# The beginning of a SwiGLU stage: a third pair's first product in front, weight sums behind the norm's lo parts, TensorE's products in order

## The chip, the cores and the metric

The kernel runs on one core of one Trainium2 chip. The metric is the device time of one execution in microseconds (us), the median of several runs. TensorE (PE) multiplies matrices, VectorE (DVE) and ScalarE (ACT) work on elements, GpSimd (POOL) does a part of that and issues some transfers, SyncE (SP) issues most loads.

## The reference

One layer of a residual block over 1024 tokens with 1024 channels: a mixing part, and then a SwiGLU feed-forward network (FFN) of width 2816. Only the FFN's beginning matters here:

```
mix = einsum('bsd,de->bse', g_a * y_a + g_b * y_b, w_o[l])
x = x + g1 * mix
h2 = rms_norm(x, norm_ffn_g[l]) * (1.0 + sc2) + sh2
a, bgate = jnp.split(jnp.einsum('bsd,df->bsf', h2, w_ffn_in[l]), 2, axis=-1)
x = x + g2 * jnp.einsum('bsf,fd->bsd', jax.nn.silu(a) * bgate, w_ffn_out[l])
return rms_norm(x, final_norm_g)
```

`a` and `bgate` have 2816 columns each, which are 22 blocks of 128.

## The kernel before

Everything is kept with channels on the 128 partitions and tokens along the free dimension, in two halves of 512 tokens. A float32 product is made of three matmuls on operands that are split into a hi part (rounded) and a lo part (the rest): weight hi by operand hi, weight hi by operand lo, weight lo by operand hi. These are lines 283, 284 and 286 in `mm3`. A weight tile of 128x1024 is split by `split_w`: ACT casts the hi (`wh`, L205), DVE subtracts to get the lo (`wl`, L206). An operand tile of 128x512 is split by `t_split` in the same way (L322 on ACT, L323 on DVE).

The FFN's first matrix is multiplied by a scheme of Strassen's kind (Winograd's form). A "dual" `d` is a pair of column blocks; it takes seven products instead of eight, in the order `PRODUCTS = "1265734"`. Each product has two parts p of 4 x 3 = 12 matmuls, 24 in all. Products 1, 6, 7 and 4 add up in the banks `x`, product 2 in `y`, 5 and 3 in `z`, two PSUM banks each. There are eleven duals.

- Product 1 takes h2 of the first half of the tokens, channel blocks 0 to 3; product 2 the same half, blocks 4 to 7. Only these two need nothing of the second half.
- Product 6 takes `t2`, products 5, 7, 3 and 4 take `t1`, `t3`, `b22` and `t4`: sums of blocks of both halves, split in hi and lo.
- Weights: products 1 and 2 take blocks 11 and 12 as loaded. Products 6, 5 and 7 need sums of blocks (L228, L229, L230), product 3 one more (L232); these are 128x1024 operations on DVE. `dual_units(..., early)` makes the seven weights of a dual. When `early` is true, each block is loaded when its product comes, so blocks 11, 12 and 22 are loaded twice; otherwise all four are loaded at product 1.

The loads go to a ring of five 128x1024 raw buffers (a sixth is added after `norm_2_last`), the split weights to three `wh` and three `wl` buffers. `next_w` writes the weights of the product two places further before it hands out the present one.

The stage before writes x1 of the second half and sums its squares. Then the order written in the code is: (0,1), written (dual, product); the second half's norm begins on PE (L404, between the two parts of (0,1)), ACT (L333) and DVE (L338 to L340), which gives `r2`; then (0,2), (1,1) and (1,2), with `norm_2_half(k, r2)` ahead of each; the fourth `norm_2_half`; `norm_2_last`; then (0,6), (0,5), (0,7), (0,3), (0,4), the same five of dual 1, and from dual 2 on seven products each. `norm_2_half` normalises block k and k + 4 (L824 on DVE, L831 on ACT), makes t2 (L850, L327) and splits it. `norm_2_last` makes and splits t1, t3 (L863), b22 and t4, in that order. So DVE has to do the norm, the operands and the weights here.

`in_evac` reads the banks: products 1, 6, 5 are copied by ACT (L905); 2, 7, 3 are added by DVE (L907, L910, L914 and L915); 4 goes through ACT's Silu (L918) and DVE (L919). After the last product of a dual, `hid_set` splits seven tiles into three staging tiles and POOL stores them.

The order in the code isn't the order on an engine. A scheduler places the instructions of each engine when the kernel is built, by the order in the code and by its own estimate of when operands are ready. Each engine then works in that order. `tc.issue_after(ins)` puts the instructions that are written under it, those on the engine of `ins`, behind `ins`.

PSUM has eight banks, six in the pool `ps` (`ps_tile`) and two in `ps2` (`ps2_tile`). Before the change, x and z of every dual come from `ps`, and y from `ps2`, except for dual 1, whose y comes from `ps` (`y_tile`).

Of the kernel before, what the change touches and what calls it, by code (L numbers as in the profile page):

```python
# [37 lines left out]
ALU = mybir.AluOpType  # L38
# [53 lines left out]

PRODUCTS = "1265734"

GROUP, GROUPS = 3, 3
# [10 lines left out]
def block_kernel(ctx: ExitStack, tc: tile.TileContext, x0, xT, c, vecs, ada, w_first, w_plain, w_duals,  # L108
                 w_short, w_conf, w_o, w_fi, w_fo, w_last, outT):
    nc = tc.nc  # L110
# [27 lines left out]
    def ps_tile(name):  # L138
        return psp.tile([P, H], F32, tag="ps", name=name)
# [13 lines left out]
    def f32(t):  # L153
        return t.bitcast(F32)
# [29 lines left out]
    def raw_tile(n=1024):  # L184

        raws.append(raws.pop(0))
        return raws[-1].tile([P, 1024], F32, tag="raw", name="raw")[:, :n]

    def load(src, n=1024):
        raw = raw_tile(n)  # L190
        nc.sync.dma_start(raw, src)
        return raw
# [6 lines left out]
    def split_w(raw, n, after=(), lo_engine=nc.vector):  # L199
        wh = whp.tile([P, 1024], F32R, tag="wh", name="wh")[:, :n]  # L200
        wl = wlp.tile([P, 1024], F32R, tag="wl", name="wl")[:, :n]
        with ExitStack() as order:
            for ins in after:
                order.enter_context(tc.issue_after(ins))
            nc.scalar.copy(wh, raw)  # L205
            lo = lo_engine.tensor_tensor(wl, raw, f32(wh), ALU.subtract)  # L206
        if n == T and lo_engine is nc.gpsimd:
            pool_los.append(lo.ins)
        return wh, wl

    def dual_units(mats, n, early=False, eng=nc.vector):

        a = {}

        def get(*blocks):
            for b in blocks:
                a[b] = load(mats[("11", "12", "21", "22").index(b)], n)

        def unit(m):
            if early:  # L220
                get(*{"1": ("11",), "2": ("12",), "6": ("21", "22", "11"), "3": ("12",), "4": ("22",)}.get(m, ()))
            elif m == "1":
                get("11", "12", "21", "22")
            if m in "12":
                return split_w(a["1" + m], n, (), eng)
            if m == "6":
                a["s1"] = a["22"] if early else raw_tile(n)
                eng.tensor_tensor(a["s1"], a["21"], a["22"], ALU.add)  # L228
                eng.tensor_tensor(a["21"], a["21"], a["11"], ALU.add)  # L229
                eng.tensor_tensor(a["11"], a["11"], a["s1"], ALU.add)  # L230
            elif m == "3":
                eng.tensor_tensor(a["12"], a["12"], a["11"], ALU.add)  # L232
            return split_w(a[{"6": "11", "5": "s1", "7": "21", "3": "12", "4": "22"}[m]], n, (), eng)

        return {m: (lambda m=m: unit(m)) for m in PRODUCTS}


    plan = [None] * KC
# [8 lines left out]
    def next_w(ahead=AHEAD):  # L247

        fetch(ahead + 1)
        return ready.pop(0)  # L250
# [24 lines left out]
    def mm3(outs, wsl, w, xs, first, last, again=False):  # L275

        if w[1] is None:
            for ps, x in zip(outs, xs):
                mm3.ins = nc.tensor.matmul(ps, w[0][:, wsl], x, start=first, stop=last).ins
            return  # L280
        wh, wl = w[0][:, wsl], w[1][:, wsl]
        for ps, (xh, xl) in zip(outs, xs):
            nc.tensor.matmul(ps, wh, xh, start=first, stop=False, skip_group_check=again)  # L283
            nc.tensor.matmul(ps, wh, xl, start=False, stop=False, skip_group_check=again)  # L284
        for ps, (xh, _) in zip(outs, xs):
            mm3.ins = nc.tensor.matmul(ps, wl, xh, start=False, stop=last, skip_group_check=again).ins  # L286
# [5 lines left out]
            mm3(outs, slice(k * P, k * P + P), w, [act[k][h] for h in hs], k == 0, k == KC - 1)  # L292
        return outs

    def product(banks, m, t, evac=None, between=None, y_tile=ps2_tile):

        w = next_w()
        b = {"1": "x", "6": "x", "7": "x", "4": "x", "2": "y", "5": "z", "3": "z"}[m]
        n = len(t)
        for p in range(2):  # L300
            if m in "125":
                banks[b, p] = (y_tile if b == "y" else ps_tile)(b)
            ps = banks[b, p]
            for k in range(n):
                c0 = (p * n + k) * P
                mm3([ps], slice(c0, c0 + P), w, [t[k]], m in "125" and k == 0, k == n - 1, m in "6734")
            if evac:
                evac(p, m, ps)
            if between and p == 0:
                between()  # L310
# [9 lines left out]

    def t_split(src, hi, lo):
        nc.scalar.copy(hi, src)  # L322
        nc.vector.tensor_tensor(lo, src, f32(hi), ALU.subtract)  # L323

    def minus(out, a, b):

# [61 lines left out]
    x = {}  # L388
# [22 lines left out]
    def uc_tile(name, n=T + CK - 1, dt=F32):  # L411
        return ucp.tile([P, T + CK - 1], dt, tag="uc", name=name)[:, :n]
# [24 lines left out]
    for k in range(0, KC, 2):  # L437
        t = uc_tile("x0", T)
# [62 lines left out]
    KH = KC // 2  # L501
# [228 lines left out]
    banks = [[ps_tile(b) for _ in range(2)] for b in "xyz"]  # L730
# [104 lines left out]
    ts = {m: [None] * (KC // 2) for m in PRODUCTS}  # L835
# [9 lines left out]
    def norm_2_half(k, r2):  # L845

        h2_of(k, 1, r2)
        b22 = h2_of(k + KH, 1, r2)
        b11, b12 = (x1[k][:, s] for s in halves)
        nc.vector.tensor_tensor(b11, b11, b12, ALU.subtract)  # L850
        t2.append(hl_tile("t2", dt=F32))
        minus(t2[k], b11, b22)
        ts["6"][k] = t_pair("t2")
        t_split(t2[k], *ts["6"][k])

    def norm_2_last():

        for k in range(KH):
            ts["5"][k] = t_pair("t1")
            t_split(x1[k][:, halves[0]], *ts["5"][k])  # L860
        for k in range(KH):
            b12, b22 = x1[k][:, halves[1]], x1[k + KH][:, halves[1]]
            nc.vector.tensor_tensor(b12, b22, b12, ALU.subtract)  # L863
            ts["7"][k] = t_pair("t3")
            t_split(b12, *ts["7"][k])
        for k in range(KH):
            ts["3"][k] = t_pair("b22")
            t_split(x1[k + KH][:, halves[1]], *ts["3"][k])
        b21 = [x1[k + KH][:, halves[0]] for k in range(KH)]
        for k in range(KH):  # L870
            minus(b21[k], t2[k], b21[k])
        for k in range(KH):
            ts["4"][k] = t_pair("t4")
            t_split(b21[k], *ts["4"][k])

    sums = {}
    for h in range(2):
# [6 lines left out]


    N_IN = FC // 2
    in_units = [dual_units([w_fi[d, m] for m in range(4)], 1024, d < 2) for d in range(N_IN)]
    in_order = [(d, m) for d in range(2) for m in "12"] + [(d, m) for d in range(2) for m in PRODUCTS[2:]]
    in_order += [(d, m) for d in range(2, N_IN) for m in PRODUCTS]
    plan += [in_units[d][m] for d, m in in_order]  # L890
    ha = {}
    in_banks = [{} for _ in range(N_IN)]

# [6 lines left out]
    def in_evac(d):  # L900
        def evac(p, m, ps):
            f = 2 * d + p
            if m in "165":
                ha[f, m] = t = in_tile(d, m)
                nc.scalar.copy(t, ps)  # L905
            elif m == "2":
                nc.vector.tensor_tensor(ha[f, "1"], ps, ha[f, "1"], ALU.add)  # L907
            elif m == "7":
                t = ha[f, "5"]
                nc.vector.tensor_tensor(t, ps, t, ALU.add)  # L910
                nc.scalar.activation(t, t, AF.Silu, scale=-1.0)
            elif m == "3":
                t = ha[f, "6"]
                nc.vector.tensor_tensor(t, ps, t, ALU.add)  # L914
                nc.vector.tensor_tensor(t, t, ha[f, "5"], ALU.mult)  # L915
            else:
                t = gip.tile([P, H], F32, tag="g", name="g4")
                nc.scalar.activation(t, ps, AF.Silu, scale=-1.0)  # L918
                nc.vector.tensor_tensor(t, t, ha[f, "1"], ALU.mult)  # L919
                ha[f, "4"] = t  # L920
        return evac
# [40 lines left out]
        to[g, m] = [t_load((g * GROUP + i, m)) for i in range(GROUP)]  # L962

    def in_product(d, m):
        product(in_banks[d], m, ts[m], in_evac(d), y_tile=ps_tile if d == 1 else ps2_tile)
        if d == N_IN - 1:
            group_load(0, m)

# [3 lines left out]

    r2 = None
    product(in_banks[0], "1", ts["1"], in_evac(0), norm_2_start)
    r2 = rstd_end(*r2)
    for i, (d, m) in enumerate(in_order[1:4]):
        norm_2_half(i, r2)
        in_product(d, m)
    norm_2_half(KH - 1, r2)
    norm_2_last()  # L980
    close(*phase_1)
    raws.append(open_pool("raw_a", 1, side="right", stack=ctx)[1])
    x1ap = open_pool("x1a", 2, side="right", stack=ctx)[1]
    phase_2 = [open_pool("gi", 7), open_pool("stage", 3, side="right")]
    gip, stagep = (p for _, p in phase_2)
    for d, m in in_order[4:]:
        in_product(d, m)
        if m == PRODUCTS[-1]:
            if 2 <= d < 6:
                for i in range(40 + 2 * (d - 2), 42 + 2 * (d - 2)):  # L990
                    modulation(i, x1ap.tile([P, T], F32, tag="x1", name="ada"))
            hid_set(d)
# [31 lines left out]
    for g in range(GROUPS):  # L1024
        for d in range(2):
            banks = {}
# [177 lines left out]
```

## Time and profile before

| | us |
|---|---|
| median of 3 runs | 1505.06 |
| lowest and highest run | 1504.25, 1505.3 |
| the profiled execution | 1502.96 |
| its span in the trace | 1501.2 |
| first product of the FFN begins on PE | 841.26 |
| first product 6 begins on PE | 864.07 |

The mean granted clock of TensorE over the whole execution is 0.995 of full speed. All rows that follow are of that one profiled execution; times in them are counted from the start of its span. A row of a timeline has the start, the duration, the engine, the line, the operation, output<-inputs, the shape and the count, and in brackets the idle time of the engine before it and what ended it. A matmul's row is longer than the step from one matmul to the next, since matmuls overlap; the step is read from the starts. The same holds, by a little, for DVE.

### The profile page before, as it was taken

What the parts mean: (1) busy time and instruction counts of PE and PEld (TensorE: products, weight loads), DVE (VectorE), ACT (ScalarE), POOL (GpSimd) and SP (SyncE); (2) the same over time, 40 slices, a digit from 0 to 9 for tenths busy, and PEclk for the clock granted to TensorE, in tenths of its full rate; (3) what the DMA queues carried; (4) which work ended last, traced back from release to release, by engine and by line L of the source; (5) the groups of instructions that cost most, each with busy time, mean ns of one, the idle gap of its engine ahead of it and who ended that gap; (6) DMA issues with size and microseconds to landing.
All of it is one profiled execution on the core that took longest, in us unless ns stands there. A gap on an engine that the chain in (4) does not pass through costs nothing.

```text
span 1501.2 us, 17711 instructions
## 1 busy us (share of the span) xinstructions
PE 1469.3 (98%) x6455; PEld 1202.0 (80%) x6455; DVE 1141.0 (76%) x1569; ACT 623.1 (42%) x896; POOL 538.2 (36%) x467
## 2 busy tenths in 40 slices
PE   6999999999999999999999989999999999999997
PEld 2788888888888788887788868888888888888887
DVE  7994999887887984777767789776666665667755
ACT  4653433443343353244345454444444443222235
POOL 0037777777767773410121001111000016444005
PEclk9999999999999999999999989999999999999999
DMA  9522223232222268555765337544444449998403
GB/s 352 207 64 74 94 71 112 70 108 75 98 71 85 99 261 299 167 175 175 231 207 183 126 98 236 200 169 153 152 149 150 153 148 351 364 324 256 141 28 112
DMA packets 82697, 247.24 MB, mean 165 GB/s; under 512 B 9521, under 2 KB 11697, under 8 KB 82610
## 3 DMA queue, kind: packets, MB, share of 16 engines
q1 hardware_dynamic: 41776, 137.91, 27.4%
q0 software_dynamic: 36944, 95.44, 19.2%
q10 hardware_dynamic: 3890, 12.78, 2.2%
q8 instruction: 50, 0.82, 0.2%
q14 instruction: 37, 0.30, 0.1%
HBM read 183.69 MB, written 62.39 MB: 164 GB/s over the span
## 4 chain that ended last, share of the span: by engine, by line
PE 93%; DVE 4%; issue 1%; ACT 1%; DMA 1%; POOL 0%; POOLq 0%; ACTq 0%; DVEq 0%
PE x L286 11%; PE x L284 11%; PE x L283 10%; PE z L283 7%; PE z L284 7%; PE z L286 7%; PE y L284 6%; PE y L283 6%; PE y L286 6%; PE ya L284 2%; PE mix L286 2%; PE mix L284 2%; PE ya L283 2%; PE ya L286 2%; PE mix L283 2%; PE yb L283 2%
## 5 line engine op out<-in xcount | busy, mean ns | idle before, releaser
L205 ACT CAST wh<-raw 128x1024 fp32r<-128x1024 f32 (+2 forms) x257 | 259.4, 1010 | 482.8 <-PE z L284 122.0
L206 POOL TENSOR_TENSOR wl<-raw,wh 128x1024 fp32r<-128x1024 f32 x92 | 227.2, 2471 | 131.1 <-ACT wh L205 130.9
L206 DVE TENSOR_TENSOR wl<-raw,wh 128x1024 fp32r<-128x1024 f32 (+2 forms) x165 | 188.4, 1142 | 52.7 <-ACT wh L205 50.0
L671 DVE SCALAR_TENSOR_TENSOR c<-diff,vec,c 128x512 f32<-128x512 f32 x248 | 178.6, 751 | 3.3
L930 POOL DMA_DIRECT2D hid<-stage x71 | 37.9, 534 | 358.7 <-DVE stage L323 353.0
L283 PE MATMUL x<-th,wh 128*128 128x512 f32 x240 | 93.4, 389 | 0.0
L284 PE MATMUL x<-tl,wh 128*128 128x512 f32 x240 | 93.4, 389 | 0.0
L286 PE MATMUL x<-th,wl 128*128 128x512 f32 x240 | 93.4, 389 | 0.0
L671 DVE SCALAR_TENSOR_TENSOR c<-u,wsum,c 128x512 f32<-128x512 f32 x112 | 84.1, 751 | 1.8
L264 DVE CUSTOM_DVE_ANT_0 raw<-raw,cs,vec 128x1024 f32<-128x1024 f32 x24 | 35.5, 1486 | 50.6 <-DMA raw<-in_ada 50.6
L283 PE MATMUL z<-th,wh 128*128 128x512 f32 x168 | 65.4, 389 | 0.0
L284 PE MATMUL z<-tl,wh 128*128 128x512 f32 x168 | 65.4, 389 | 0.0
L286 PE MATMUL z<-th,wl 128*128 128x512 f32 x168 | 65.4, 389 | 0.0
L228 POOL TENSOR_TENSOR raw<-raw 128x1024 f32<-128x1024 f32 x12 | 29.8, 2482 | 95.0 <-DVE wl L206 94.2
L322 ACT CAST stage<-g 128x512 fp32r<-128x512 f32 x62 | 38.3, 621 | 52.0 <-DMA hid<-stage 25.1
L323 DVE TENSOR_TENSOR stage<-g,stage 128x512 fp32r<-128x512 f32 x62 | 42.5, 688 | 20.5 <-ACT stage L322 20.4
L956 POOL DMA_DIRECT2D th<-hid x71 | 38.1, 537 | 52.0 <-PE x L286 28.3
L283 PE MATMUL yb<-zsh,wh 128*128 128x512 f32 x128 | 50.0, 391 | 2.8 <-DVE gb L793 2.8
L283 PE MATMUL x<-t2h,wh 128*128 128x512 f32 x120 | 47.7, 400 | 5.1 <-ACT wh L205 2.8
L286 PEld LDWEIGHTS x<-th,wl 128*128 128x128 f32 x240 | 45.1, 188 | 9.4
L283 PEld LDWEIGHTS x<-th,wh 128*128 128x128 f32 x240 | 45.1, 188 | 9.3
L284 PEld LDWEIGHTS x<-tl,wh 128*128 128x128 f32 x240 | 45.1, 188 | 9.3
(1012 smaller groups left out, 4263.8 us busy)
## 6 DMA issues: line engine op xcount, KB each, us to landing
hid<-stage POOLq DMA_DIRECT2D x71, 512.0 KB, 4.0
raw<-in_w_fi SPq DMA_DIRECT2D x50, 512.0 KB, 4.3
raw<-in_w_duals SPq DMA_DIRECT2D x48, 512.0 KB, 3.5
th<-hid POOLq DMA_DIRECT2D x71, 256.0 KB, 5.9
tl<-hid POOLq DMA_DIRECT2D x71, 256.0 KB, 6.0
ada<-in_ada SPq DMA_DIRECT2D x24, 512.0 KB, 5.8
raw<-in_ada SPq DMA_DIRECT2D x24, 512.0 KB, 4.5
raw<-in_w_fo SPq DMA_DIRECT2D x24, 384.0 KB, 6.2
```

The costliest lines, as they stand in the source:

```text
L205: nc.scalar.copy(wh, raw)
L206: lo = lo_engine.tensor_tensor(wl, raw, f32(wh), ALU.subtract)
L228: eng.tensor_tensor(a["s1"], a["21"], a["22"], ALU.add)
L264: nc.vector.tensor_tensor_reduce(out=raw, in0=raw, in1=cs, scale=1.0, scalar=col(V_ADA, b), op0=ALU.mult, op1=ALU.add, accum_out=modc(b),)
L283: nc.tensor.matmul(ps, wh, xh, start=first, stop=False, skip_group_check=again)
L284: nc.tensor.matmul(ps, wh, xl, start=False, stop=False, skip_group_check=again)
L286: mm3.ins = nc.tensor.matmul(ps, wl, xh, start=False, stop=last, skip_group_check=again).ins
L322: nc.scalar.copy(hi, src)
L323: nc.vector.tensor_tensor(lo, src, f32(hi), ALU.subtract)
L671: tap.ins = nc.vector.scalar_tensor_tensor(out=out, in0=src[:, s : s + H], scalar=wt, in1=acc, op0=ALU.mult, op1=ALU.add).ins
L930: nc.gpsimd.dma_start(hid_dram[key], s)
L956: nc.gpsimd.dma_start(t, hid_dram[key][:, s])
```

## The change

A constant `FRONT = 3` says how many duals have their first products in front. The order becomes (0,1), (0,2), (1,1), (1,2), (2,1), then the rest of dual 0, of dual 1 and of dual 2 (from product 2), and from there as before. Dual 2's weights are made with `early`, too. A `norm_2_half` stands ahead of each of the four products behind (0,1), (2,1) among them. The evacuation of (2,1) is left to the time just ahead of (2,2), so x of dual 2 stays in its two banks until then.

y of dual 1 comes from `ps2` now, as all y do, and z of dual 0 from `ps2` instead of `ps`.

The weight of product 6 of duals 1 and 2 is written under `issue_after` with the last DVE instruction of `norm_2_last` (the last t4l): its three sums and its lo stand behind it in DVE's order. The products 6 of duals 1 and 2 are written under `issue_after` with the last matmul of the product before them in the code, so PE's order can't put them ahead of it.

```
+FRONT = 3
...
-    def product(banks, m, t, evac=None, between=None, y_tile=ps2_tile):
+    def product(banks, m, t, evac=None, between=None, y_tile=ps2_tile, z_tile=ps_tile):
...
-                banks[b, p] = (y_tile if b == "y" else ps_tile)(b)
+                banks[b, p] = {"x": ps_tile, "y": y_tile, "z": z_tile}[b](b)
...
-        nc.vector.tensor_tensor(lo, src, f32(hi), ALU.subtract)
+        t_split.ins = nc.vector.tensor_tensor(lo, src, f32(hi), ALU.subtract).ins
...
             t_split(b21[k], *ts["4"][k])
+        norm_2_last.ins = t_split.ins
...
-    in_units = [dual_units([w_fi[d, m] for m in range(4)], 1024, d < 2) for d in range(N_IN)]
-    in_order = [(d, m) for d in range(2) for m in "12"] + [(d, m) for d in range(2) for m in PRODUCTS[2:]]
-    in_order += [(d, m) for d in range(2, N_IN) for m in PRODUCTS]
-    plan += [in_units[d][m] for d, m in in_order]
+    in_units = [dual_units([w_fi[d, m] for m in range(4)], 1024, d < FRONT) for d in range(N_IN)]
+    in_order = [(d, m) for d in range(FRONT) for m in "12"][: 2 * FRONT - 1]
+    in_order += [(d, m) for d in range(N_IN) for m in PRODUCTS if (d, m) not in in_order]
+
+    def in_unit(d, m):
+
+        if d in range(1, FRONT) and m == "6":
+            with tc.issue_after(norm_2_last.ins):
+                return in_units[d][m]()
+        return in_units[d][m]()
+
+    plan += [lambda d=d, m=m: in_unit(d, m) for d, m in in_order]
...
-        product(in_banks[d], m, ts[m], in_evac(d), y_tile=ps_tile if d == 1 else ps2_tile)
+        product(in_banks[d], m, ts[m], in_evac(d) if (d, m) != (FRONT - 1, "1") else None,
+                z_tile=ps2_tile if d == 0 else ps_tile)
...
-    for i, (d, m) in enumerate(in_order[1:4]):
+    for i, (d, m) in enumerate(in_order[1 : 2 * FRONT - 1]):
         norm_2_half(i, r2)
         in_product(d, m)
-    norm_2_half(KH - 1, r2)
     norm_2_last()
...
-    for d, m in in_order[4:]:
-        in_product(d, m)
+    for d, m in in_order[2 * FRONT - 1 :]:
+        if (d, m) == (FRONT - 1, "2"):
+            for p in range(2):
+                in_evac(d)(p, "1", in_banks[d]["x", p])
+        if d in range(1, FRONT) and m == "6":
+            with tc.issue_after(mm3.ins):
+                in_product(d, m)
+        else:
+            in_product(d, m)
```

## The prediction

> **What bounds the kernel now.** I read the page's busy times first, then TensorE's (PE's) waits, then stretches of the FFN's beginning, then the order of PE's, VectorE's (DVE's) and ScalarE's (ACT's) instructions there.
>
> ```profile
> span 1501.2 us, 17711 instructions
> PE 1469.3 (98%) x6455; PEld 1202.0 (80%) x6455; DVE 1141.0 (76%) x1569; ACT 623.1 (42%) x896; POOL 538.2 (36%) x467
> ```
> ```profile
> PE yb L283 <- DVE gb L793: 2.8, 2, 1.6
> PE x L283 <- ACT wh L205: 2.8, 1, 2.8
> PE x L283 <- ACT t2h L322: 2.3, 1, 2.3
> PE x L286 <- DVE wl L206: 1.0, 1, 1.0
> ```
> PE is busy nearly throughout, so only its gaps and its slow phases can be won; work of other engines counts where PE waits for it. Three of these waits lie in the stage that the change touches (x is a bank of products 1, 6, 7, 4; t2 the operand of product 6). The stretches around them (columns: length, busy time with count for PE, its weight loads, DVE, ACT, POOL; granted clock; DMA share; GB/s):
>
> ```profile
> 841.26:868.39 27.13, 27.13 (x117) 21.36 (x115) 25.58 (x35) 15.30 (x23) 0.54 (x1) 1.00 0.33 104
> 868.39:876.20 7.81, 5.41 (x16) 3.80 (x16) 7.76 (x13) 4.81 (x10) 0.00 (x0) 0.78 0.00 1
> 885.59:896.50 10.91, 7.06 (x19) 5.07 (x19) 9.46 (x14) 7.12 (x11) 0.00 (x0) 0.69 0.29 93
> 896.50:930.00 33.50, 33.50 (x149) 27.77 (x148) 27.69 (x39) 15.05 (x22) 4.78 (x9) 1.00 0.76 254
> 930.00:1469.30 539.30, 539.30 (x2391) 447.15 (x2391) 373.03 (x467) 200.31 (x284) 112.63 (x212) 1.00 0.59 192
> ```
> In the second and third stretch PE idles and then runs at a reduced granted clock; after 896.5 it is busy to 1469 without a gap, so what is won here reaches the end. How much there is to win comes from PE's rows at the borders:
>
> ```profile
> 841.26 0.39 PE L283 MATMUL x<-h20h,wh 128*128 128x512 f32 x1
> ...
> 843.75 0.39 PE L286 MATMUL x<-h23h,wl 128*128 128x512 f32 x1
> ...
> 864.07 0.39 PE L283 MATMUL x<-t2h,wh 128*128 128x512 f32 x1
> ...
> 868.16 0.39 PE L286 MATMUL x<-t2h,wl 128*128 128x512 f32 x1
> 870.83 0.73 PE L283 MATMUL x<-t2h,wh 128*128 128x512 f32 x2 [2.28 <-ACT t2h L322]
> ...
> 876.20 0.39 PE L286 MATMUL z<-t1h,wl 128*128 128x512 f32 x1
> ...
> 885.36 0.40 PE L286 MATMUL x<-t3h,wl 128*128 128x512 f32 x1
> 888.57 0.50 PE L283 MATMUL x<-t2h,wh 128*128 128x512 f32 x1 [2.81 <-ACT wh L205]
> ...
> 889.37 0.49 PE L284 MATMUL x<-t2l,wh 128*128 128x512 f32 x1
> 890.89 0.79 PE L286 MATMUL x<-t2h,wl 128*128 128x512 f32 x1 [1.03 <-DVE wl L206]
> ...
> 896.50 0.40 PE L286 MATMUL x<-t2h,wl 128*128 128x512 f32 x1
> 896.73 0.39 PE L283 MATMUL z<-b22h,wh 128*128 128x512 f32 x1
> ```
> From the first two rows, eleven steps in 2.49 us: a matmul takes 0.226 us of PE, a product of 24 matmuls 5.43 us. From 868.16 to 876.20 stand 15 matmuls, which need 3.40 of 8.04 us: 4.64 lost, of which 2.44 (868.39 to 870.83) are the gap and 2.20 the slow phase behind it. From 885.36 to 896.50 stand 18, which need 4.08 of 11.14 us: 7.06 lost, of which 2.98 and 1.29 are gaps and 2.79 slow phase. Together **11.7 us** are lost here. The rows also tell why. The first gap waits for the last t2, the end of the second norm's chain. The second is product (1,6), which PE's order has put ahead of (0,3): z<-b22 follows only at 896.73. PE stands before weights that aren't split yet, and cannot go on to (0,3).
>
> What DVE did in that time (starts, durations):
>
> ```profile
> 848.28 0.68 DVE L338 SCALAR_TENSOR_TENSOR r2t<-r2r 128x512 f32<-128x512 f32 x1
> ...
> 871.25 0.68 DVE L323 TENSOR_TENSOR t2l<-t,t2h 128x512 fp32r<-128x512 f32 x1
> ...
> 882.67 1.22 DVE L228 TENSOR_TENSOR raw<-raw 128x1024 f32<-128x1024 f32 x1
> 883.81 0.69 DVE L323 TENSOR_TENSOR t3l<-x,t3h 128x512 fp32r<-128x512 f32 x1
> 884.41 1.22 DVE L229 TENSOR_TENSOR raw<-raw 128x1024 f32<-128x1024 f32 x1
> ...
> 886.14 1.22 DVE L230 TENSOR_TENSOR raw<-raw 128x1024 f32<-128x1024 f32 x1
> ...
> 887.88 1.22 DVE L232 TENSOR_TENSOR raw<-raw 128x1024 f32<-128x1024 f32 x1
> ...
> 889.62 1.22 DVE L206 TENSOR_TENSOR wl<-raw,wh 128x1024 fp32r<-128x1024 f32 x1
> ...
> 891.36 2.49 DVE L323 TENSOR_TENSOR t4l<-x,t4h 128x512 fp32r<-128x512 f32 x4
> ```
> By the starts, a 128x1024 operation holds DVE for 1.14 us and a 128x512 one for 0.60. Dual 1's weight sums (L228 to L232) and its lo (L206) stand between the lo parts that (0,3) and (0,4) need, and ahead of t4l, which ends at 891.36 + 4 x 0.60 = 893.8.
>
> **The change part by part.** *The third dual's product 1* adds no matmul. It brings 5.43 us of PE work, ready since the first half's norm, ahead of (0,6). From (1,2)'s end at 864.07, PE without waits would begin (0,6) at 869.5, (0,5) at 874.9, (0,7) at 880.4, (0,3) at 885.8, (0,4) at 891.2 and (1,6) at 896.7. As in the trace of before, where 18 matmuls of (0,6) ran ahead of the gap, the last t2 is then needed at 869.5 + 18 x 0.226 = 873.6. It was ready at 871.25 + 0.60 = 871.85. Ahead of it on DVE now comes the lo of weight (2,1), 1.14: 873.0. That leaves 0.6 us, so no gap, if nothing else moves.
>
> Something else may. The fifth early weight takes the fifth raw buffer, so (0,6)'s loads go one buffer further round, and the last of them waits for the lo of (1,1):
>
> ```profile
> 842.36 1.23 DVE L206 TENSOR_TENSOR wl<-raw,wh 128x1024 fp32r<-128x1024 f32 x1
> ```
> ```profile
> raw<-in_w_fi SPq DMA_DIRECT2D x8, 512.0 KB, 3.4
> ```
> It lands at 842.36 + 1.23 + 3.4, about 847.0, so two of (0,6)'s sums and the one of (0,3) (a buffer further still) can fall behind the start of the norm's chain, where before DVE had time. That is 0 to 3 x 1.14 = 3.4 us later for the last t2, 876.4 at worst, a wait of 0 to 2.8. Against it, L338 stood at 848.28 behind such sums, and can come sooner without them; hence I take a small part of the bound.
>
> *The sums behind the lo parts.* Four sums and one lo, 5 x 1.14 = 5.7 us, leave the queue ahead of t4l, and 1.14 is added: t4l ends at 893.8 - 5.7 + 1.14 = 889.2, or at 892.6 by the 3.4 above. Behind the new wait stand, on DVE, dual 1's sums and its lo; ACT's cast waits for them:
>
> ```profile
> 887.47 1.05 ACT L205 CAST wh<-raw 128x1024 fp32r<-128x1024 f32 x1 [3.98 <-DVE raw L230]
> ```
> Three sums (3.4), the cast (1.05) and the lo (1.2) make weight (1,6) ready between 894.9 and 898.3, and its hi 1.2 earlier. PE needs the hi at 896.7 and the lo 0.45 later: a wait of 0 to 1.2. (2,6)'s sums come far behind t4l anyway: nothing.
>
> *PE in order.* (0,3) and (0,4), 10.9 us, go ahead of (1,6), and hide its sums; without that cover (the trace of before) the wait was 2.98 + 1.29 with 2.79 of slow phase. Their own operands come at 0.60 each, four per product with one weight lo: 3.5 us of DVE against 5.43 of PE.
>
> *Banks.* y of dual 1 and z of dual 0 now use the pair of y of dual 0. The latter is read early enough, and (1,1) lies between:
>
> ```profile
> 850.88 0.68 DVE L907 TENSOR_TENSOR g<-y,g 128x512 f32<-128x512 f32 x1
> ```
> Dual 2's x stays unread in two banks until (2,2), so z of dual 1 gets the banks of x of dual 0, freed by the last evacuation of (0,4); (1,6), 5.43 us, lies between. Two ACT copies move with it, no more. Cost 0; the rival below is what happens otherwise.
>
> *Loads.* Dual 2 loads three blocks again, 1.57 MB on SP's queue. In the stretch from 896.5 to 930 the share is 0.76 at 254 GB/s; at 254/0.76 = 334 GB/s they need 4.7 us of the 8.0 us that are free there. Hidden, 0; without that cover the products of dual 2 would wait up to 4.7.
>
> *Sum.* Won: 4.64 + 7.06 = 11.7. Kept: between 0 and 2.8 + 1.2 = 4.0 of waits; with no row nearer to either end I take the middle, 2.0. Gain 9.7 us: the profiled execution goes from 1502.96 (span 1501.2) to 1493.3. That execution is 2.1 below the median; the same gain on the median gives 1505.06 - 9.7 = **1495.4**.
>
> *Whether a short wait costs more than itself.* A PE wait elsewhere kept its clock:
>
> ```profile
> 716.92 0.50 PE L283 MATMUL yb<-zsh,wh 128*128 128x512 f32 x1 [1.60 <-DVE gb L793]
> ```
> ```profile
> 715.00:720.00 5.00, 3.40 (x15) 2.55 (x14) 3.69 (x6) 1.66 (x3) 1.08 (x2) 1.00 0.48 161
> ```
> So 1.60 us cost no clock (1.00 granted) and 2.28 did (0.78 over the stretch). My residual is made of waits below 1.6 and carries no slow phase. [...]
>
> **The rivals.** *One gap stays long (0.18).* If (0,6)'s sums stand ahead of L338 or among the halves of the norm, the last t2 comes at the late bound, 2.8 us late, and the clock falls as it did: 4.6 to 7.1 of the 11.7 stay, 7.1 to 4.6 are won, 1498.0 to 1500.5. For it: the scheduler's order put sums ahead of L338 before too. Against it: those sums now come later in the program than three of the four halves.
>
> *Both gaps come back at their old price (0.07).* The lead of 5.43 us is eaten by DVE, and (1,6) waits behind t4l instead of in front of it: 1505.1, no change. It decides at 5 us of further DVE work ahead of the last t2; I count 1.1 to 4.6.
>
> *The parked banks bite (0.10): slower.* z of dual 1 can't start before ACT has read both x banks of (0,4). ACT works in order, and a cast into a staging tile can stand ahead of that read, waiting for a store:
>
> ```profile
> 905.15 0.60 ACT L918 ACTIVATE g<-x 128x512 f32<-128x512 f32 x1 [1.90 <-PE x L286]
> ...
> 919.80 0.62 ACT L322 CAST stage<-g 128x512 fp32r<-128x512 f32 x1 [2.89 <-DMA hid<-stage]
> ```
> With seven stores and three staging tiles, four casts wait: 4 x 2.89 = 11.6, and a slow phase of 2.8 makes 14.4; with my 2.0 kept and 11.7 won that is +4.7, about 1509.8. It decides only from a delay of 5.43 us on. Against it: the read came as soon as its bank was done, and no store was ahead of it.
>
> **How the numbers follow.** The forecast has 0.65 with its bounds, 1493.4 (nothing kept) to 1497.4 (4.0 kept). About 0.2% (3.0 us) is what a measurement of this kernel can tell from no change. The forecast and the first rival are faster than 1502.05: 0.83; the second is the same, 0.07; the third slower, 0.10. The range reaches from 1493.0 (0.4 for the spread of the runs) over the first rival to 1501.0; outside lie the other two.
>
> **What would show it.** Right: PE shows x of dual 2 ahead of x<-t2, z<-b22 and x<-t4 ahead of the second group of x<-t2; no wait over 1.6 us between 864 and 905; granted clock 1.00 throughout; L228 to L230 behind t4l; products that ended at 930 end some 10 us sooner. Wrong: a PE wait on t2h or wh of over 2 us with the clock below 1.00 behind it (first rival); PE's z waiting for ACT L918 around 902 (the third); DVE waiting for a load ahead of L338.

## The result and the profile after

| | us |
|---|---|
| before, median of 5 runs | 1505.13 (1504.25 to 1505.64) |
| after, median of 5 runs | 1498.32 (1497.93 to 1498.95) |
| ratio, 95% interval | 0.9956, 0.9943 to 0.997 |
| profiled execution after, its span | 1498.83, 1497.1 |

The change makes the kernel 6.8 us faster. The forecast was 9.7 us and 1495.4, with bounds of 1493.4 to 1497.4; the range was 1493.0 to 1501.0. In the changed kernel's code the matmuls of `mm3` stand in lines 286, 287 and 289 (283, 284 and 286 before); L231 to L235 are the weight sums (L228 to L232), L341 is the old L338, L917 the old L905. In the experiments they shift by a few lines more; the tiles name the work.

First the page, then PE's waits (total, times, longest), whose only rows over 3 us after the first 100 us are these:

```profile
span 1497.1 us, 17720 instructions
PE 1467.0 (98%) x6455; PEld 1201.2 (80%) x6455; DVE 1140.8 (76%) x1569; ACT 623.8 (42%) x896; POOL 537.7 (36%) x467
```
```profile
PE yb L286 <- DVE gb L796: 3.5, 2, 1.8
PE z L286 <- ACT g L917: 3.2, 1, 3.2
```
The waits on t2h, wh and wl at the FFN's beginning are gone. In their place stands one that wasn't there: z, the banks of products 5 and 3, waits for ACT's copy. The stretches show how clean the rest is (columns as in the prediction):

```profile
869.50:876.00 6.50, 6.50 (x29) 5.10 (x29) 6.50 (x11) 4.18 (x7) 0.00 (x0) 1.00 0.26 82
885.00:897.00 12.00, 8.85 (x27) 6.74 (x27) 11.80 (x16) 8.58 (x15) 0.00 (x0) 0.72 0.68 220
897.00:910.00 13.00, 13.00 (x59) 10.78 (x58) 13.00 (x19) 6.35 (x10) 0.54 (x1) 1.00 0.56 180
910.00:925.00 15.00, 15.00 (x68) 12.43 (x67) 11.66 (x17) 8.07 (x13) 3.92 (x8) 1.00 1.02 348
```
Only the stretch from 885 to 897 has idle time and a reduced clock. PE's rows there:

```profile
887.10 0.39 PE L289 MATMUL x<-t3h,wl 128*128 128x512 f32 x1
890.64 0.80 PE L286 MATMUL z<-b22h,wh 128*128 128x512 f32 x1 [3.15 <-ACT g L917]
...
896.72 0.39 PE L289 MATMUL z<-b22h,wl 128*128 128x512 f32 x1
...
898.99 0.39 PE L286 MATMUL x<-t4h,wh 128*128 128x512 f32 x1
...
904.43 0.39 PE L286 MATMUL x<-t2h,wh 128*128 128x512 f32 x1
```
(0,3) could begin at 887.10 + 0.23 = 887.33 and begins at 890.64: 3.31 us. The 14 matmuls up to 896.72 take 6.08 us instead of 3.17: 2.91 of slow phase. So 6.2 of the 11.7 us stay. The order is the one the change asks for: z<-b22, x<-t4, and only then x<-t2 of dual 1, without a wait.

What the copy waited for is read from ACT's order and, in the second view, from DVE's, where the sum stands (L235) that released ACT's first cast:

```profile
883.95 1.05 ACT L208 CAST wh<-raw 128x1024 fp32r<-128x1024 f32 x1 [3.74 <-DVE raw L235]
884.91 0.62 ACT L325 CAST b22h<-x 128x512 fp32r<-128x512 f32 x1
885.43 1.05 ACT L208 CAST wh<-raw 128x1024 fp32r<-128x1024 f32 x1
886.38 1.65 ACT L325 CAST b22h<-x 128x512 fp32r<-128x512 f32 x3
887.94 2.17 ACT L325 CAST t4h<-x 128x512 fp32r<-128x512 f32 x4
890.02 1.05 ACT L917 COPY g<-z 128x512 f32<-128x512 f32 x2
```
```profile
849.36 1.23 DVE L232 TENSOR_TENSOR raw<-raw 128x1024 f32<-128x1024 f32 x1 [3.07 <-DMA raw<-in_w_fi]
...
851.76 0.68 DVE L341 SCALAR_TENSOR_TENSOR r2t<-r2r 128x512 f32<-128x512 f32 x1
...
874.29 0.67 DVE L326 TENSOR_TENSOR t2l<-t,t2h 128x512 fp32r<-128x512 f32 x1
...
882.65 1.21 DVE L235 TENSOR_TENSOR raw<-raw 128x1024 f32<-128x1024 f32 x1
...
889.73 2.49 DVE L326 TENSOR_TENSOR t4l<-x,t4h 128x512 fp32r<-128x512 f32 x4
```
ACT stood idle for 3.74 us before the cast of weight (0,3), because the sum for it (L235) ran at 882.65; behind that cast came a second weight's cast, b22h, t4h and only then the copy that frees z. That sum had moved. In the trace of before it stood ahead of the norm's chain (the first of the stage's L232 rows, one for each dual in turn):

```profile
847.14 1.23 DVE L232 TENSOR_TENSOR raw<-raw 128x1024 f32<-128x1024 f32 x1 [0.56 <-DMA raw<-in_w_fi]
```
My theory (A) was that the gap of 3.3 us is the copy's place in ACT's order, and that the held cast and the t4h casts each put about 2 us to it. The rivals: the operands of (0,3) are late anyway (B); DVE as a whole is the limit, and what is taken from one wait comes back at the next (F); the held cast alone decides, and the place of the copies does not (G); the orderings alone are the whole gain (C); the third dual brings nothing (D); with PE's order fixed, the place of the sums is of no account (E).

### The profile page after: what moved, and what is told of

The parts are those of the page before. It is cut to its first block, busy times and chain, and to the rows that moved or that the text cites. A ratio compares the mean times of both kernels' runs of the same rounds, so it can differ in the third digit from the quotient of the medians.

```text
span 1497.1 us, 17720 instructions
## 1 busy us (share of the span) xinstructions
PE 1467.0 (98%) x6455; PEld 1201.2 (80%) x6455; DVE 1140.8 (76%) x1569; ACT 623.8 (42%) x896; POOL 537.7 (36%) x467
## 4 chain that ended last, share of the span: by engine, by line
PE 91%; DVE 5%; issue 1%; DMA 1%; ACT 1%; POOL 0%; POOLq 0%; ACTq 0%; DVEq 0%
PE x L286 10%; PE x L289 10%; PE x L287 10%; PE z L286 7%; PE z L287 7%; PE z L289 7%; PE y L286 6%; PE y L289 6%; PE y L287 6%; PE ya L289 2%; PE ya L286 2%; PE ya L287 2%; PE mix L286 2%; PE mix L287 2%; PE mix L289 2%; PE yb L289 2%
## 5 line engine op out<-in xcount | busy, mean ns | idle before, releaser
L231 POOL TENSOR_TENSOR raw<-raw 128x1024 f32<-128x1024 f32 x12 | 29.8, 2483 | 95.1 <-DVE wl L209 94.3
L286 PE MATMUL y<-th,wh 128*128 128x512 f32 x132 | 51.3, 389 | 0.0
```

## The experiments

All times are medians. The kernel before ran beside each of the three groups of experiments, with medians of 1504.06, 1504.38 and 1504.36; each ratio goes against the one beside it. A ratio is given with its 95% interval, and is not exactly the quotient of the two medians.

**The changed kernel again.** No edit.

> The changed kernel once more, on the chip of the runs beside it: 5 to 7 us below the kernel before, with the gap of about 3.3 us ahead of (0,3) at the same place, PE released by ScalarE's copy of z. If the slow clock behind a gap of this length comes only at times, the time behind the gap is either as before (2.9 us lost) or near nothing.

1499.43, ratio 0.9962 (0.9949 to 0.9974). The gap is there again:

```profile
891.41 0.79 PE L286 MATMUL z<-b22h,wh 128*128 128x512 f32 x1 [3.19 <-ACT g L917]
```
```profile
885.00:897.00 12.00, 8.81 (x28) 6.76 (x27) 11.97 (x17) 9.35 (x15) 0.00 (x0) 0.72 0.75 243
```
The slow clock came again too (0.72).

**The orderings alone**, on the kernel before:

```
+        if (d, m) == (1, "6"):                    # both the weight unit and the product
+            with tc.issue_after(...): ...          # last t4l (DVE), last matmul of (0,4) (PE)
```


> The kernel before with four products in front, as it was, and only the two orderings of the change for dual 1: the sums of (1,6) behind the last t4l, PE's (1,6) behind (0,4). Theory A: the first gap stays as before (2.4 us and 2.2 us of slow clock), the wait for the weight of (1,6) goes, and PE waits for the copies of z ahead of (0,3) instead: 1499 to 1503. Rival C (the orderings alone are the whole gain): 1498 to 1499 as the changed kernel.

1502.61, ratio 0.9991 (0.9982 to 1.0): a gain of 1.5 us, just at the edge of what can be told. The first gap stayed; the wait for weight (1,6) went; the copy of z held PE for 0.60 us only. The sum of (0,3) stands early here, as in the kernel before, so ACT cast that weight early, too, and came to the copies at 885.81:

```profile
872.06 0.74 PE L283 MATMUL x<-t2h,wh 128*128 128x512 f32 x2 [2.28 <-ACT t2h L322]
...
886.43 0.50 PE L283 MATMUL z<-b22h,wh 128*128 128x512 f32 x1 [0.60 <-ACT g L914]
```
```profile
872.06:877.00 4.94, 4.80 (x19) 3.37 (x20) 4.94 (x9) 4.00 (x8) 0.00 (x0) 1.00 0.00 0
```
```profile
848.37 1.23 DVE L232 TENSOR_TENSOR raw<-raw 128x1024 f32<-128x1024 f32 x1 [0.55 <-DMA raw<-in_w_fi]
```
```profile
879.65 1.05 ACT L205 CAST wh<-raw 128x1024 fp32r<-128x1024 f32 x1 [1.55 <-issue]
...
885.81 1.06 ACT L914 COPY g<-z 128x512 f32<-128x512 f32 x2
```
So C falls. The orderings alone don't bring the long gap at z. What the third dual brings is the late sum of (0,3): 882.65 in the changed kernel, 882.95 and 881.96 in the next two experiments, which have the third dual, too. The slow phase behind the first gap was missing in this execution (granted clock 1.00): it was the fastest of the eleven, at 1499.88, so its trace shows less loss than the median has. It also has a wait that the changed kernel hasn't, 1.72 us at 960.11 on an addition of DVE.

**The third dual alone**, the changed kernel without both orderings:

```
-            with tc.issue_after(norm_2_last.ins):
-                return in_units[d][m]()
...
-            with tc.issue_after(mm3.ins):
-                in_product(d, m)
```


> The changed kernel without the two orderings: the third dual's product 1 in front, banks and early loads as changed, but sums and PE's products placed freely. Theory A: the first gap is gone (4.6 us won), (1,6) is again placed ahead of (0,3) and waits for its weight with slow clock behind it, as before: 1499.5 to 1501.5. Rival D (the third dual brings nothing, since VectorE gets as much more to do): 1504 to 1506.

1506.98, ratio 1.002 (1.0011 to 1.0029): slower, and neither theory had that. The first gap is gone, as A said. But (1,6) ahead of (0,3) now costs 7.00 us of waiting and not 2.81:

```profile
894.73 0.79 PE L286 MATMUL x<-t2h,wh 128*128 128x512 f32 x1 [7.00 <-ACT wh L208]
```
```profile
893.63 1.05 ACT L208 CAST wh<-raw 128x1024 fp32r<-128x1024 f32 x1 [4.25 <-DVE raw L233]
```
PE comes to that point without the delay of the first gap, and the weight is ready later than before. By the trace that cancels the gain: product (2,2) begins 94.2 us after the FFN's first product, 94.9 in the kernel before. What makes the kernel slower stands later, in dual 2: waits of 1.43 us at 954.44, on a copy of ACT, and of 0.64 on the weight lo behind it, where the kernel before has none.

**Without the ordering of the sums**, the rest as changed:

```
-        if d in range(1, FRONT) and m == "6":
-            with tc.issue_after(norm_2_last.ins):
-                return in_units[d][m]()
```


> The changed kernel without the ordering of the sums: dual 1's sums and lo may stand among the norm's lo parts again; PE's order stays (0,3), (0,4), (1,6). Theory A: the cast of weight (1,6) now stands among the t4h casts on ScalarE, ahead of the copies of z, and waits for VectorE's sums; the gap ahead of (0,3) grows from 3.3 to 5 to 7 us, the loss in the stage by 2 to 4 us: 1500.5 to 1503. Rival E (with PE's order fixed the place of the sums is of no account): the time of the changed kernel, 1497.5 to 1499.

1505.41, ratio 1.001 (1.0001 to 1.0019). The direction of A, the size beyond it: the cast of (1,6) among the t4h casts waits 4.25 us for its sums, and the copy of z behind it holds PE for 8.50:

```profile
892.63 1.04 ACT L208 CAST wh<-raw 128x1024 fp32r<-128x1024 f32 x1 [4.25 <-DVE raw L233]
893.58 1.13 ACT L325 CAST t4h<-x 128x512 fp32r<-128x512 f32 x2
894.62 1.06 ACT L914 COPY g<-z 128x512 f32<-128x512 f32 x2
```
```profile
895.25 0.79 PE L286 MATMUL z<-b22h,wh 128*128 128x512 f32 x1 [8.50 <-ACT g L914]
```
E falls. PE's products stand in the order (0,3), (0,4), (1,6) here, so the ordering of the sums matters by what it takes out of ACT's way. This kernel and the one before it differ only by PE's ordering, and their intervals overlap: without the ordering of the sums it only changes which product waits. With it, PE's ordering adds nothing: the changed kernel built without `issue_after` in the products has the same order of instructions on every engine (read from the built programs; it wasn't run).

**The copies first**, b22 and t4 both split behind product (0,5):

```
+    def norm_2_rest():           # b22, t4: the second half of norm_2_last
...
+    for d, m in in_order[2 * FRONT - 1 : 2 * FRONT + 1]:
+        in_product(d, m)
+    norm_2_rest()
```


> b22 and t4 are split behind product (0,5) in the code, so ScalarE's two copies of z of dual 0 stand ahead of the b22h and t4h casts; all else as in the changed kernel. Theory A (the gap of 3.3 us ahead of (0,3) and the 2.9 us of slow clock behind it come from these copies standing behind eight casts): the gap goes or falls under 1 us, granted clock 1.00 between 885 and 897, about 6 us less than the changed kernel, 1492 to 1494. Rival B (the operands b22 or weight (0,3) are late anyway): a wait of 2 us or more stays, now on b22 or wl, and the time stays at 1497 to 1499.

1498.29, ratio 0.9959 (0.9946 to 0.9973): the changed kernel's time, and not the 1492 to 1494 that A gave. The gap ahead of (0,3) went (0.53 us on a b22l), so B falls; but DVE's evacuations now stand among the lo parts and wait for PE, t4l and the sums behind it come later, and PE waits at (1,6), with the clock at 0.79:

```profile
894.48 0.69 DVE L928 TENSOR_TENSOR g<-z,g 128x512 f32<-128x512 f32 x1 [0.99 <-PE z L289]
```
```profile
902.71 0.50 PE L286 MATMUL x<-t2h,wh 128*128 128x512 f32 x1 [2.15 <-ACT wh L208]
```
```profile
900.00:908.00 8.00, 5.85 (x19) 4.34 (x18) 8.00 (x11) 5.55 (x8) 1.07 (x2) 0.79 0.38 130
```
Here F holds: the loss moved on by two products.

**The sum early**, only the sum of (0,3) written with the weight of (0,5):

```
+            if soon and m == "5":
+                get("12")
+                eng.tensor_tensor(a["12"], a["12"], a["11"], ALU.add)
```


> Only the sum for weight (0,3) is written earlier, with the weight of (0,5), ahead of norm_2_last; the copies of z keep their place behind t4h. Theory A1 (ScalarE stood 3.7 us before the cast of (0,3), which waited for that sum, and all casts and the copies behind it came late by that): copies of z about 3 us earlier, the gap under 0.5 us, 1492 to 1494. Rival A2 (the place behind b22h and t4h alone makes the copies late, since those wait for VectorE and for buffers): gap of 2 us or more, 1496 to 1499.

1498.38, ratio 0.9964 (0.9951 to 0.9977). No wait of PE ahead of (0,3) is listed any more, as A1 said, but the time is the changed kernel's and misses A1's 1492 to 1494. Smaller waits came: 0.86 us ahead of a matmul of (0,7) and 0.70 of (1,6), both for a lo, and in (1,3) 1.03 for a copy of z and 0.65 for a lo. These 3.24 us are about the length of the gap that went; what they don't bring is a slow phase (the clock is 1.00 in every stretch from 842 to 930), and by the trace the stage is 1.5 us shorter. So F holds here in good part. The profiled execution also lost some clock outside the stage (its mean is 0.997, against 0.999 with the modulation late too; ahead of the FFN it has a wait of 2.51 us at 714.41), so I take no size from its time.

```profile
885.44 0.50 PE L292 MATMUL x<-t3h,wl 128*128 128x512 f32 x1 [0.86 <-DVE wl L209]
...
902.65 0.50 PE L292 MATMUL x<-t2h,wl 128*128 128x512 f32 x1 [0.70 <-DVE wl L209]
```

**t4 late.** One edit to the changed kernel, that of the copies first, but for t4 alone:

```
+    def norm_2_t4(b21):          # only the four splits of t4
...
+    for d, m in in_order[2 * FRONT - 1 : 2 * FRONT + 1]:
+        in_product(d, m)
+    norm_2_t4(b21)
```


> The changed kernel with one edit: t4 alone is split behind product (0,5) in the code, so on ScalarE the copies of z stand ahead of the four t4h casts, but still behind the cast of weight (0,3), which waits for its late sum, and behind b22h. Theory A: t4h accounts for 2.1 us of the 3.3, the rest stays: PE waits 1.0 to 1.6 us ahead of (0,3), without slow clock, released by the copy of z; 2 to 4 us less than the changed kernel, 1495 to 1497. Rival G (the held cast alone decides, the copies' place does not): the gap stays near 3 us and the time within 1 us of the changed kernel. Rival F (what is taken here comes back at weight (1,6)): no gap here, one of 2 us or more ahead of (1,6).

1495.43, ratio 0.9942 (0.9929 to 0.9956). Only the place of t4 differs from the changed kernel, and A's numbers came: the cast of (0,3) is still held, the copy stands at 888.28, PE waits 1.14 us ahead of (0,3), at full clock (1.00), and 0.71 ahead of (1,6):

```profile
884.29 1.05 ACT L208 CAST wh<-raw 128x1024 fp32r<-128x1024 f32 x1 [3.71 <-DVE raw L235]
...
888.28 1.06 ACT L921 COPY g<-z 128x512 f32<-128x512 f32 x2
```
```profile
888.91 0.50 PE L286 MATMUL z<-b22h,wh 128*128 128x512 f32 x1 [1.14 <-ACT g L921]
900.83 0.50 PE L286 MATMUL x<-t2h,wh 128*128 128x512 f32 x1 [0.71 <-ACT wh L208]
```
```profile
885.00:897.00 12.00, 10.86 (x48) 8.64 (x47) 11.94 (x18) 8.85 (x15) 0.00 (x0) 1.00 0.54 154
```
G falls, and F as a rule: what comes back at (1,6) is 0.71.

**The sum early and the modulation late.** As the early sum, and the modulation products (a 1.28 us DVE operation that stood among the sums of (1,6)) behind the stores of the dual before:

```
+                    with tc.issue_after(t_split.ins):
+                        modulation(...)
```


> As the run with the early sum of (0,3), and the modulation products moved behind the stores: the gap ahead of (0,3) stays at 0.3 us, the wait for the lo of (1,6), 0.9 us there, falls under 0.3 us, as 1.2 us of VectorE work goes from among the sums; theory A: 1495.5 to 1497.5. Rival F: within 1 us of the changed kernel.

1496.72, ratio 0.9942 (0.9929 to 0.9954), 2.7 us below the changed kernel beside it. The wait for weight (1,6) is gone as expected; 0.88 us in (0,7) and 0.73 in (1,3) are left. So the two edits together pay as t4 late does; the modulation late without the early sum was not run.

**All three**: t4 late, the sum early, the modulation late.

> The changed kernel with three edits: the sum of (0,3) written early; t4 alone (not b22) split behind product (0,5), so the copies of z stand ahead of t4h on ScalarE; the modulation products behind the stores of the dual before, so none stands among the sums of (1,6). Theory A: no gap over 1 us ahead of (0,3), the wait for weight (1,6) under 1 us, 2 to 4 us below the changed kernel: 1494.5 to 1496.5. Rival F (VectorE as a whole is the limit there, so whatever is taken from one wait comes back at the next): within 1 us of the changed kernel.

1494.83, ratio 0.9935 (0.9922 to 0.9947), 4.6 below the changed kernel beside it: it beats both kernels. PE's waits in the stage are 0.87 us in (0,7) and 0.71 ahead of (1,6), the clock is 1.00:

```profile
885.83 0.50 PE L292 MATMUL x<-t3h,wl 128*128 128x512 f32 x1 [0.87 <-DVE wl L209]
...
902.25 0.50 PE L289 MATMUL x<-t2h,wh 128*128 128x512 f32 x1 [0.71 <-ACT wh L208]
```
```profile
885.00:897.00 12.00, 11.18 (x49) 9.27 (x50) 12.00 (x18) 8.55 (x15) 0.00 (x0) 1.00 0.42 131
```
Against t4 late alone, by the ratios, it can't be told apart.

The FFN begins at another time in each execution (841.3 to 843.8), so sizes are best counted from there. ACT's copy of z begins 47.98 us behind the FFN's first product in the changed kernel, 45.98 with the sum early, 45.69 with t4 late and 44.16 with all three: the late sum and the t4h casts put about 2 us each to the copy, as A said. By the same count product (2,2) begins at 94.9 before, 89.6 in the changed kernel, 89.4 with the copies first, 88.1 with the sum early, 86.0 with the modulation late too, 85.8 with all three and 85.7 with t4 late.

## Why the prediction was right, and where not

Two of the three parts of the mechanism came as forecast, the third did not, and its loss is why 6.8 us were won and not 9.7.

*The first gap* went, as forecast. (0,6) ran without a listed wait. Two of (0,6)'s sums did fall ahead of the norm's chain and waited 3.07 us for a load, which the prediction had named as a sign of being wrong; L341 stood at 851.76, where L338 stood at 848.28. The FFN began 0.78 us later in this execution (842.04 instead of 841.26), so 2.7 us of that belong to the change. The last t2 was ready at 874.29 + 0.60 = 874.9, 874.1 on the scale of before: between the 873.0 and the 876.4 of the prediction. The slack was enough.

*The sums behind the lo parts*: t4l ended at 889.73 + 4 x 0.60 = 892.1, 891.3 on the scale of before, within 889.2 to 892.6. (1,6) had no wait, but its cover was 6 us longer than planned, because PE was late. Where PE came on time (t4 late; all three) it waited 0.71, within the 0 to 1.2 allowed.

*PE in order* is the step that failed. It counted the operands of (0,3) on DVE, 3.5 us against 5.43, and nothing else. (0,3) adds to the banks of (0,5), and can't start before ACT has copied them (3.15 us waited for L917); and ACT copies them only behind the cast of weight (0,3), b22h and t4h. In the trace of before the copy ran late, too:

```profile
888.95 2.17 ACT L322 CAST t4h<-x 128x512 fp32r<-128x512 f32 x4
891.03 1.06 ACT L905 COPY g<-z 128x512 f32<-128x512 f32 x2
```
That is later than 885.6, when PE would have come to (0,3): (1,6), placed ahead, had hidden it. The row was there to read, but it didn't give the price. The cast that held ACT there (887.47, 3.98 us) was that of (1,6), which the change moves away; with the orderings alone the copy came at 885.81 and cost 0.60. In the changed kernel another cast holds ACT, that of (0,3), since its sum went from 847.14 to 882.65. The prediction saw that this sum could fall behind the start of the norm's chain, but priced it as DVE time ahead of t2 alone, not as a weight that comes late and holds ACT. Why the scheduler put it so far back no run shows; written one product earlier, it stood at 871.64 without a wait for its load.

The price was 3.31 us and 2.91 of slow phase, against a residual of 2.0 in the sum. That residual, meant for t2 and (1,6), was 0 for both. With 6.2 kept, 11.7 - 6.2 = 5.5 us of gain stand in the two traces' stage. The medians differ by 6.8, but the two profiled executions by only 4.1: that of before was 2.1 below its median and that of after 0.5 above. So the traces can't show where the difference between 5.5 and 6.8 lies. Two of the prediction's signs of being right failed with this step: there is a wait of over 1.6 us between 864 and 905, and the clock is below 1.00 behind it (0.72 from 885 to 897).

*The sum's 11.7* held as a ceiling: no kernel here gains more, and t4 late and all three gain 8.93 and 9.55 us over the kernel before beside them, close to the forecast's 9.7. With the copies out of the way the forecast's mechanism is worth about what it said.

*The first rival* gave 1498.0 to 1500.5 for one long gap with slow clock behind it, and the time lies there. Its mechanism (a late t2) is not what happened. The time missed the forecast's own bounds by 0.9 us and stayed in the range because that was drawn wide enough for a rival; that another gap of about the same price came in its place is luck. *The parked banks* cost nothing: no wait for L930 (the old L918) is listed. *The loads* were hidden: between 910 and 925 the DMA share was 1.02, and PE busy throughout. *Both gaps at their old price* is near what the third dual does alone (1506.98), or with PE's ordering but without that of the sums (1505.41); the orderings alone gain 1.5 us. The two parts need each other.

## What to carry to other kernels

Before a product is moved forward on a full engine, list everything it waits for at its new place, the read of the bank that it writes included, and look up in the old trace when each of these ran; a late one may have been hidden by the very wait that is taken away. When a change moves an operation, follow it to everything that waits for it, not only to the engine whose time it takes. A cast that waits for another engine held every evacuation behind it in its engine's order here: a late sum on VectorE (3.74 us idle on ScalarE) and four casts not yet needed (2.17 us) stopped TensorE, two engines away, for 3.15 us. What helped here was to write the less urgent splits later, and only so many of them (t4, not b22 and t4) that VectorE doesn't begin to wait itself: with both late it waited 0.90 and 0.99 us for TensorE between 880 and 908, with t4 alone not at all between 884 and 905.

## What the runs showed of the hardware

In these traces the slow clock behind a PE gap isn't fixed by the gap's length alone. The same gap on t2 (2.28 us waited) ended in a stretch at 0.78 in the trace of before, and at 1.00 in that of the orderings alone; a wait of 2.15 was followed by 0.79, and one of 2.95 by no slow clock (1.00). In the changed kernel's second trace, in the stage ahead:

```profile
714.25 0.50 PE L286 MATMUL yb<-zsh,wh 128*128 128x512 f32 x1 [2.95 <-DVE gb L796]
```
```profile
714.00:718.00 4.00, 3.24 (x13) 2.37 (x13) 2.91 (x6) 1.24 (x2) 1.51 (x3) 1.00 0.98 351
```
And with the three edits, at the same place, with a wait of 3.07:

```profile
714.00:718.00 4.00, 3.15 (x7) 2.51 (x8) 3.20 (x6) 1.24 (x2) 1.61 (x3) 0.59 0.91 336
```
Waits of PE between 100 and 1470 us, by length, each with the granted clock of a stretch that has the matmuls behind it:

| wait, us | trace | granted clock | stretch |
|---|---|---|---|
| 1.60 | before | 1.00 | 715 to 720 |
| 1.67 | changed kernel | 1.00 | 717.69 to 722 |
| 1.81 | changed kernel | 1.00 | 712.78 to 717.5 |
| 2.15 | copies first | 0.79 | 900 to 908 |
| 2.28 | before | 0.78 | 868.39 to 876.2 |
| 2.28 | orderings alone | 1.00 | 872.06 to 877 |
| 2.81, and 1.03 close behind | before | 0.69 | 885.59 to 896.5 |
| 2.90 | sum early, modulation late | 1.00 | 714 to 718 |
| 2.95 | changed kernel again | 1.00 | 714 to 718 |
| 3.07 | all three | 0.59 | 714 to 718 |
| 3.15 | changed kernel | 0.72 | 885 to 897 |
| 3.19 | changed kernel again | 0.72 | 885 to 897 |
| 7.00 | third dual alone | 0.67 | 885 to 900 |
| 8.50 | without the ordering of the sums | 0.67 | 885 to 900 |

In these rows the clock is 1.00 with each wait of up to 1.81, below 1.00 with three of the six from 2.15 to 2.95, and below 1.00 with all five from 3.07 to 8.50. The prediction took 1.60 and 2.28 as the ends between which the clock falls; the two rows of 2.28 and those of 2.90 and 2.95 show that a wait as long as the upper end, or longer, can keep its clock. In the three cases that were worked out here the slow phase cost 2.20 to 2.91 us.
